# A diffusion backbone's last stage on one core: the half of the tokens that it begins with, and where a norm's sums stand among the last products

## Chip, core and metric

One core of a Trainium2 chip runs the whole kernel. The metric is the device time in microseconds (us), the median of several runs; the profile is one further execution. The engines are named TensorE (PE in the rows), VectorE (DVE), ScalarE (ACT), GpSimd (POOL) and SyncE (SP, which here only issues DMAs). Each engine takes its instructions strictly in the order in which the program gives them, and waits at one whose inputs are not there.

## What is computed

One layer of the backbone over 1024 tokens of 1024 channels: an adaptive norm, a two-directional diagonal state-space scan with a gate, and then the squared-ReLU MLP and a final norm, which is all that the change touches:

```python
def _rmsnorm(x, g):
    xf = x.astype(jnp.float32)
    y = xf * lax.rsqrt(jnp.mean(xf * xf, axis=-1, keepdims=True) + EPS)
    return (y * g.astype(jnp.float32)).astype(x.dtype)

def _mlp(h, w1, b1, w2, b2):
    a = jax.nn.relu(h @ w1 + b1)
    return (a * a) @ w2 + b2

# in reference(), D_FF = 4096:
        x = x + g2 * _mlp(_modulate(_rmsnorm(x, norm2_g[i]), sh2, sc2),
                          mlp_w1[i], mlp_b1[i], mlp_w2[i], mlp_b2[i])
    return _rmsnorm(x, final_g)
```

## The kernel before

Channels lie on the 128 partitions, in eight blocks `d`, tokens along the free dimension. `acc[:, d]` holds the running result x of block d for all 1024 tokens; `halves` are tokens 0 to 511 and 512 to 1023. Every float32 product is made of three matmuls (`mm3`, lines 783 to 785) of operands split in a rounded part and a rest: rounded x rounded, rounded x rest, rest x rounded. ScalarE makes the rounded part (`rounded`, line 937), VectorE or GpSimd subtracts to get the rest (`rest`, line 934).

The order of the work is written out by hand: the schedule is manual, and what the program lists first an engine does first.

The MLP's second product has 32 blocks of 128 hidden channels. The first 30 go through a seven-product scheme (Strassen's), in 70 steps, `t` = 0 to 69, of the loop at line 1444. Step t takes u = t // 14, one of seven products i and a quarter q of the output channels. Its parts:

- `y_rests(t)`: VectorE's rests of the activations that were rounded in step t - 1, among them, in steps 66 and 67, the rests of the weights `w2_last(0)` and `w2_last(1)` (128x1024 each).
- `product2(t)`: 18 matmuls of 512 columns, nine into the PSUM bank 2t mod 8 and nine into the next.
- `after2(t)`: VectorE takes the two banks into `acc` (`add_out`, line 1364) and, for some i, into a sum M or M into `acc`. For u = 4 that is four VectorE instructions at i = 0, 1, 3 and 5, two at i = 2 and 6, six at i = 4. The last steps are t = 62, 63 (i = 3), 64, 65, 66 (i = 4, 5, 6 of quarter 0) and 67, 68, 69 (i = 4, 5, 6 of quarter 1). Products i = 5 and 6 add to the first half of the tokens alone, so steps 68 and 69 no longer touch the second half.
- `beside(t)`: the loads (SyncE), the rounding for later steps (ScalarE), GpSimd's rests and sums of the weights. `plan(t, g, t_load)` puts an activation block g into these lists: loaded in step t_load, rounded in t, its rest in t + 1. Blocks 105 to 108 are the last two blocks of hidden channels, 105 and 106 for the first half of the tokens (`aa`), 107 and 108 for the second (`ab`).

The last stage, from line 1451 on, does the other two hidden blocks directly and the final norm:

- `m2_(toks, ds, aa)` makes, for each channel block d, six matmuls into a bank and one VectorE instruction (line 1463) that adds the bank to `acc`. `m2_sq` does that for each d and has ScalarE square the result (line 978) and VectorE or GpSimd add the square to a sum (line 979). Squares and adds are 512 columns wide for a half, 256 for a quarter of the tokens.
- `norm_cols` sums over the partitions by tiny matmuls (line 1001), and VectorE and ScalarE turn the sums into reciprocal roots with a Newton step (lines 1004 to 1013): one VectorE instruction, the root on ScalarE, four VectorE instructions. It is a generator: nothing is issued before its first `next`, which issues all up to the root.
- `norm_rows` spreads the roots over the partitions by matmuls into a PSUM bank (line 1019).
- `last` scales a block by gain and root on VectorE (line 1479) and, every second block, has SyncE issue the store (line 1475). For the last quarter ScalarE applies the gain (line 1516) ahead of time, and VectorE multiplies by the root (line 1520).

The order before: the first half is done whole (512 columns), with its adds on VectorE; then comes the third quarter of the tokens, with the first half's norm made beside it and the adds on GpSimd; then the fourth quarter, with the first half's eight `last` between its pieces; then the third quarter's eight `last`; then the fourth quarter's norm and store.

Of the kernel before, what the change touches and what calls it, by code (L numbers as in the profile page):

```python
# [47 lines left out]
def kernel(ctx, tc, cst, bc, x, xl, ada_w, glu_w, w1, w2, out):  # L48
# [41 lines left out]
    def bank(i, n=512, o=0):  # L90
        return PS[:, 512 * i + o:512 * i + o + n]
# [690 lines left out]
    def mm3(o, wt, xt, start, stop):  # L782
        PE.matmul(o, wt[0], xt[0], start=start, stop=False)  # L783
        PE.matmul(o, wt[0], xt[1], start=False, stop=False)  # L784
        PE.matmul(o, wt[1], xt[0], start=False, stop=stop)  # L785
# [146 lines left out]
    def rest(to, src, eng=V, *dims):  # L932
        hi, lo = (vw(v[:, 0:size(dims)], *dims) for v in to) if dims else to
        eng.tensor_tensor(lo, src, hi.bitcast(F32), op=OP.subtract)  # L934

    def rounded(to, src, *dims):
        S.copy(vw(to[0][:, 0:size(dims)], *dims) if dims else to[0], src)  # L937
# [34 lines left out]
    def sum_sq(d, toks, eng=None):  # L972
        n, ss = toks.stop - toks.start, sq_sum(toks)
        if d == 0:
            S.activation(ss, acc[:, d, toks], AF.Square)
        else:
            sq = tmp()[:, 0:n]
            S.activation(sq, acc[:, d, toks], AF.Square)
            (eng or P).tensor_tensor(ss, ss, sq, op=OP.add)
# [16 lines left out]
    def norm_cols(b, toks=halves[0]):  # L996

        n, ss = (toks.stop - toks.start) // 128, sq_sum(toks)
        cols = bank(b, n)
        for c in range(n):  # L1000
            PE.matmul(cols[:, c:c + 1], ss[:, 128 * c:128 * c + 128], one, start=True, stop=True)
        v, r, t = (C("ldt")[:, 12 * nn[0] + 4 * i:12 * nn[0] + 4 * i + n] for i in range(3))
        nn[0] += 1
        V.tensor_scalar(v, cols, 1.0 / D, EPS, op0=OP.mult, op1=OP.add)
        S.activation(r, v, AF.Sqrt)
        yield r
        V.reciprocal(r, r)
        yield
        V.scalar_tensor_tensor(t, v, -0.5, r, op0=OP.mult, op1=OP.mult)
        yield  # L1010
        V.tensor_tensor(t, t, r, op=OP.mult)
        yield
        V.scalar_tensor_tensor(r, t, 1.5, r, op0=OP.add, op1=OP.mult)
# [288 lines left out]
    def w2_last(f):  # L1302
        o = 1024 + 2048 * f
        return at(W, o, 1024), at(W, o + 1024, 1024)
# [4 lines left out]
    def plan(t, g, t_load):  # L1309
        loads.setdefault(t_load, []).append(g)  # L1310
        rounds.setdefault(t, []).append(g)
        rests.setdefault(t + 1, []).append(g)
# [5 lines left out]
            t = 14 * (u - 1)  # L1318
            plan(t + 8 + 2 * m // 3, 21 * u + m, t + (1, 2, 4, 6, 8, 12, 13)[0 if m < 5 else 1 + (m - 5) // 3])
    for m in range(4):  # L1320
        plan(66 + m // 2, 105 + m, 64)

    def beside(t):

        for g in loads.get(t, ()):
            load_y(g)
        if t == -6:
            load_w2(0, range(3, 4))
        elif t == -5:
            load_w2(1, (0, 2, 3, 1))  # L1330
        elif t in (-2, 0):
            i = t // 2 + 1
            SP.dma_start(out=acc[:, 6 + i], in_=RD[0].rearrange("(p a c) -> p a c", p=128, a=2)[:, i])
        round2(t + 3)
        for g in rounds.get(t, ()):
            to = y_slot(g)
            rounded(to, to[1].bitcast(F32))
        if t in (65, 66):
            rounded(w2_last(t - 65), w2_raw[:, t - 65])
        rest2(t + 3)  # L1340
        sum2(t + 4)
        if t == 62:
            SP.dma_start(out=w2_raw, in_=w2v[:, 30:32])

    def y_rests(t):
        for g in rests.get(t, ()):
            to = y_slot(g)
            rest(to, to[1].bitcast(F32))
        if t in (66, 67):
            rest(w2_last(t - 66), w2_raw[:, t - 66])  # L1350

    def bank2(p, n):
        return bank((2 * p + n) % 8)

    def product2(p):
        u, q, i = L2[p]
        hi, lo = (vw(v, 3, 2, 128) for v in slot2(p))
        for n in range(2):
            for m in range(3):
                mm3(bank2(p, n), (hi[:, m, n], lo[:, m, n]), y_slot(21 * u + 3 * i + m), m == 0, m == 2)  # L1360

# [4 lines left out]
    def after2(p):  # L1366
        u, q, i = L2[p]
        for n in range(2):
            d, o = 2 * q + n, bank2(p, n)
            m = at(M, 512 * d, 512)  # L1370
            if i == 0 and u == 0:
                S.copy(m, o)
            elif i in (0, 2):
                V.tensor_tensor(m, m, o, op=OP.add)
            for r, hf in (((0, 0),), ((0, 1), (1, 1)), (), ((0, 1),), ((1, 1), (1, 0)), ((0, 0),), ((1, 0),))[i]:
                add_out(o, d + 4 * r, hf)
            if u == 4 and i in (3, 4, 5):
                add_out(m, d + 4 * (i > 3), (1, 1, 0)[i - 3])
# [61 lines left out]
            S.activation(acc[:, b - 3], acc[:, b - 3], AF.Identity, bias=g2b2[:, b - 3:b - 2])  # L1440


    M = sp.tile([128, 2048], F32, name="M", tag="r2_7")
    for t in range(len(L2)):
        y_rests(t)
        product2(t)
        after2(t)
        beside(t)


    first, toks = halves[0], (slice(512, 768), slice(768, 1024))

    def m2_(toks, ds, aa, o_=0):
        w = [w2_last(f) for f in range(2)]
        n = toks.stop - toks.start
        ts = slice(o_, o_ + n)
        for f in range(2):
            for d in ds:
                ds_ = slice(128 * d, 128 * d + 128)
                mm3(bank(4 + d % 4, n), (w[f][0][:, ds_], w[f][1][:, ds_]), (aa[f][0][:, ts], aa[f][1][:, ts]), f == 0, f == 1)  # L1460
        for d in ds:
            o = acc[:, d, toks]
            V.scalar_tensor_tensor(o, bank(4 + d % 4, n), g2[:, d:d + 1], o, op0=OP.mult, op1=OP.add)  # L1463

    def m2_sq(toks, ds, aa, o_=0, eng=None):

        for d in ds:
            m2_(toks, [d], aa, o_)
            if d:
                sum_sq(d - 1, toks, eng)  # L1470
        if d == 7:
            sum_sq(7, toks, eng)
# [9 lines left out]

    ring = places[:3]
    aa, ab = ([y_slot(105 + 2 * hf + f) for f in range(2)] for hf in range(2))
    m2_sq(first, range(8), aa, eng=V)
    m2_(toks[0], range(4), ab)
    n1 = norm_cols(1, first)
    r_ = next(n1)
    for d in range(8):
        if d > 3:  # L1490
            m2_(toks[0], [d], ab)
        sum_sq(d, toks[0])
        next(n1, 0)
        if d == 5:
            rb = norm_rows(r_, 2, first)
    n1 = norm_cols(1, toks[0])
    for d in range(8):
        m2_sq(toks[1], [d], ab, 256)
        last(d, first, rb)
        if d == 2:  # L1500
            r_ = next(n1)
        elif d > 2:
            next(n1, 0)
    rb = norm_rows(r_, 3, toks[0])
    for d in range(4):
        last(d, toks[0], rb)
    n1 = norm_cols(1, toks[1])
    r_ = next(n1)
    last(4, toks[0], rb)
    for _ in n1:  # L1510
        pass
    for d in range(5, 8):
        last(d, toks[0], rb)
    for d in range(8):
        o = acc[:, d, toks[1]]
        S.activation(o, o, AF.Identity, scale=C("fg")[:, d:d + 1])
# [67 lines left out]
```

## Time and profile before

| what | us |
|---|---|
| median of 3 runs (1076.04 to 1077.04) | 1076.48 |
| the profiled execution: its own time | 1074.8 |
| the profiled execution: its span, first to last instruction | 1073.0 |
| busy in the span: TensorE | 954.5 |
| busy in the span: VectorE | 884.0 |
| busy in the span: GpSimd | 599.7 |
| busy in the span: ScalarE | 552.9 |

The share of busy time is a mean over stages with different limits, so the end of the span is to be read by itself: for every engine its instructions in order of time, and for each the idle time before it and what ended that. A row gives the start in us from the span's start, the duration, the engine, the line of the kernel, the operation, the result and its operands by tile name (T holds `acc` and the small vectors, PS is PSUM, UT the sum of squares, W and z the split activations and weights), the shapes, and a count where equal neighbours are merged; then the whole stretch is given. An instruction's duration reaches some 0.08 us into the next one on VectorE, and a matmul's even further, so that the step from start to start is the price of one in a run of equals.

### The profile page before, as it was taken

How to read it: one execution, taken by the hardware profiler on the slowest of the kernel's cores; microseconds unless marked ns; L12 is line 12 of the kernel's file. 1: busy time of each engine (PE TensorE's matmuls, PEld its weight loads, DVE VectorE, ACT ScalarE, POOL GpSimd, SP SyncE). 2: the span in 40 equal slices, each digit the busy share in tenths (PEclk: the TensorE clock that was granted, in tenths of full speed). 3: DMA queues.
4: the chain of work that ended last, by engine and by line, in shares of the span. 5: the costliest groups of instructions: out<-in, count | busy, mean ns of one | idle time of the engine just before them, and what ended most of it. 6: DMA issues, size and time to landing. Idle time of an engine off the chain costs nothing.

```text
span 1073.0 us, 15268 instructions
## 1 busy us (share of the span) xinstructions
PE 954.5 (89%) x5276; PEld 783.5 (73%) x5276; DVE 884.0 (82%) x1393; ACT 552.9 (52%) x1015; POOL 599.7 (56%) x411
## 2 busy tenths in 40 slices
PE   4788895656999998899999999998999999999995
PEld 4466674446888776588888888886678888888875
DVE  8799998999946776978665656656899999999997
ACT  6367683346973466656565554545444334343413
POOL 2868999735653814264232232324888787878603
PEclk9969797777999988999999999999999999999998
DMA  9514554775778211165545344469363535451204
GB/s 384 216 46 154 186 155 117 194 212 144 227 243 284 66 40 59 49 207 188 184 138 178 126 162 152 138 203 329 121 224 103 194 120 177 133 162 40 79 1 157
DMA packets 104782, 168.85 MB, mean 157 GB/s; under 512 B 7681, under 2 KB 61953, under 8 KB 103425
## 3 DMA queue, kind: packets, MB, share of 16 engines
q1 hardware_dynamic: 100272, 153.20, 43.6%
q10 hardware_dynamic: 4432, 14.68, 4.1%
q8 instruction: 41, 0.67, 0.3%
q14 instruction: 37, 0.29, 0.1%
HBM read 120.40 MB, written 47.45 MB: 156 GB/s over the span
## 4 chain that ended last, share of the span: by engine, by line
PE 54%; DVE 24%; ACT 8%; issue 5%; POOL 4%; DMA 4%; SPq 1%; DVEq 0%; ACTq 0%; POOLq 0%
PE PS L784 15%; PE PS L785 15%; PE PS L783 15%; DVE T L1364 3%; DVE X L476 2%; PE PS L154 2%; DVE X L475 2%; DMA DY<-X 1%; DVE z L934 1%; DVE PS L474 1%; DVE PS L473 1%; DVE W L934 1%; DVE PS L710 1%; PE PS L573 1%; PE PS L495 1%
## 5 line engine op out<-in xcount | busy, mean ns | idle before, releaser
L783 PE MATMUL PS<-z,W 128*128 128x512 f32 (+1 forms) x432 | 168.6, 390 | 2.9 <-DVE T L1184 1.5
L784 PE MATMUL PS<-z,W 128*128 128x512 f32 (+1 forms) x432 | 167.5, 388 | 2.5 <-DVE z L934 2.5
L785 PE MATMUL PS<-z,W 128*128 128x512 f32 (+1 forms) x404 | 156.7, 388 | 1.3 <-POOL W L934 1.2
L1364 DVE SCALAR_TENSOR_TENSOR T<-PS,T 128x512 f32<-128x512 f32 x160 | 112.1, 739 | 2.4 <-PE PS L785 2.2
L783 PEld LDWEIGHTS PS<-z,W 128*128 128x128 f32 x432 | 81.7, 189 | 21.2 <-DVE T L1463 2.2
L784 PE MATMUL PS<-W 128*128 128x512 f32 (+1 forms) x244 | 93.9, 385 | 3.4 <-DVE W L934 3.2
L784 PEld LDWEIGHTS PS<-z,W 128*128 128x128 f32 x432 | 81.7, 189 | 19.8 <-DVE z L934 3.7
L783 PE MATMUL PS<-W 128*128 128x512 f32 (+1 forms) x244 | 93.3, 382 | 0.0
L785 PEld LDWEIGHTS PS<-z,W 128*128 128x128 f32 x404 | 76.3, 189 | 17.9 <-POOL W L934 2.1
L934 DVE TENSOR_TENSOR z<-z 128x512 fp32r<-128x512 f32 x60 | 81.2, 1378 | 6.0 <-ACT z L937 6.0
L785 PE MATMUL PS<-W 128*128 128x512 f32 (+1 forms) x216 | 82.7, 383 | 1.5 <-POOL W L934 1.5
L785 PE MATMUL PS<-z,A 128*128 128x512 f32 x208 | 81.3, 391 | 2.5 <-POOL A L934 2.5
L934 DVE TENSOR_TENSOR W<-W 128x512 fp32r<-128x512 f32 x49 | 74.2, 1537 | 7.2 <-ACT W L937 7.2
L1212 POOL TENSOR_TENSOR T<-T 128x512 f32<-128x512 f32 x27 | 39.2, 1453 | 68.8 <-ACT T L1155 60.7
L785 PE MATMUL PS<-W,A 128*128 128x512 f32 x184 | 71.7, 390 | 0.3 <-POOL A L934 0.3
L783 PE MATMUL PS<-z,A 128*128 128x512 f32 x180 | 70.2, 390 | 0.0
L784 PE MATMUL PS<-z,A 128*128 128x512 f32 x180 | 70.0, 389 | 0.0
L1184 DVE TENSOR_TENSOR T<-T,PS 128x512 f32<-128x512 f32 x64 | 42.9, 685 | 32.4 <-PE PS L785 31.6
L937 ACT CAST W<-T 128x512 fp32r<-128x512 f32 (+1 forms) x46 | 33.0, 718 | 65.2 <-POOL T L1283 46.2
L937 ACT CAST W<-UT 128x512 fp32r<-128x512 f32 (+2 forms) x50 | 35.7, 714 | 58.6 <-POOL UT L1283 37.7
L495 PE MATMUL PS<-X,E 128*64 128x160 f32 x256 | 50.4, 339 | 14.5 <-DVE X L457 8.2
L783 PE MATMUL PS<-W,A 128*128 128x512 f32 x156 | 60.7, 389 | 0.0
(330 smaller groups left out, 2725.1 us busy)
## 6 DMA issues: line engine op xcount, KB each, us to landing
YD<-T SPq DMA_DIRECT2D x88, 256.0 KB, 2.3
z<-YD SPq DMA_DIRECT2D x60, 256.0 KB, 3.6
W<-YD SPq DMA_DIRECT2D x49, 256.0 KB, 4.2
T<-in_w_dram SPq DMA_DIRECT2D x9, 1024.0 KB, 5.8
T<-in_ada_w_dram ACTq DMA_DIRECT2D x17, 512.0 KB, 4.0
UT<-in_w_dram SPq DMA_DIRECT2D x8, 1024.0 KB, 5.9
T<-in_w_dram SPq DMA_DIRECT2D x20, 384.0 KB, 3.4
UT<-in_w_dram SPq DMA_DIRECT2D x15, 384.0 KB, 4.2
```

The costliest lines, as they stand in the source:

```text
L154: PE.matmul(ssq, C("sel"), a[:, g], start=(j, g) == (0, 0), stop=(j, g) == (7, 7))
L475: lambda: eng.tensor_tensor(out_, out_, ta, op=OP.add),
L476: lambda: eng.tensor_tensor(out_, out_, tb_, op=OP.add)]
L495: PE.matmul(b[0:64, c], e[:, g, c, 0:64], uj[:, g], start=True, stop=True)
L783: PE.matmul(o, wt[0], xt[0], start=start, stop=False)
L784: PE.matmul(o, wt[0], xt[1], start=False, stop=False)
L785: PE.matmul(o, wt[1], xt[0], start=False, stop=stop)
L934: eng.tensor_tensor(lo, src, hi.bitcast(F32), op=OP.subtract)
L937: S.copy(vw(to[0][:, 0:size(dims)], *dims) if dims else to[0], src)
L1184: V.tensor_tensor(to, x_, o, op=OP.add)
L1212: P.tensor_tensor(o, x_, z_, op=op)
L1364: V.scalar_tensor_tensor(o, src, g2[:, d:d + 1], o, op0=OP.mult, op1=OP.add)
```

## The change

The last stage takes the second half of the tokens whole and the first half in two quarters, and its start moves ahead of steps 68 and 69 of the second product. The adds to the sum of squares of the half stay on VectorE, those of the quarters on GpSimd. The column sums of the half's norm are issued between the two nine-matmul groups of step 68, the rest of its chain after step 68's product, its rows between the two groups of step 69. The half's eight `last` stand thus: one ahead of the first quarter, four among its pieces, one among those of the second quarter, two behind it. For this the weights' and the second half's activations are loaded, rounded and split earlier, and banks are numbered anew. No instruction of any engine is added or removed but for the order; the same matmuls, additions, squares and stores are issued. The diff:

```diff
@@ -1318,7 +1318,7 @@
             t = 14 * (u - 1)
             plan(t + 8 + 2 * m // 3, 21 * u + m, t + (1, 2, 4, 6, 8, 12, 13)[0 if m < 5 else 1 + (m - 5) // 3])
     for m in range(4):
-        plan(66 + m // 2, 105 + m, 64)
+        plan(64 if m > 1 else 66, 105 + m, 60)
     def beside(t):
@@ -1335,8 +1335,8 @@
         for g in rounds.get(t, ()):
             to = y_slot(g)
             rounded(to, to[1].bitcast(F32))
-        if t in (65, 66):
-            rounded(w2_last(t - 65), w2_raw[:, t - 65])
+        if t in (64, 65):
+            rounded(w2_last(t - 64), w2_raw[:, t - 64])
         rest2(t + 3)
         sum2(t + 4)
         if t == 62:
@@ -1346,16 +1346,18 @@
         for g in rests.get(t, ()):
             to = y_slot(g)
             rest(to, to[1].bitcast(F32))
-        if t in (66, 67):
-            rest(w2_last(t - 66), w2_raw[:, t - 66])
+        if t in (65, 66):
+            rest(w2_last(t - 65), w2_raw[:, t - 65])
     def bank2(p, n):
         return bank((2 * p + n) % 8)
-    def product2(p):
+    def product2(p, between=None):
         u, q, i = L2[p]
         hi, lo = (vw(v, 3, 2, 128) for v in slot2(p))
         for n in range(2):
+            if n and between:
+                between()
             for m in range(3):
                 mm3(bank2(p, n), (hi[:, m, n], lo[:, m, n]), y_slot(21 * u + 3 * i + m), m == 0, m == 2)
@@ -1440,27 +1442,20 @@
             S.activation(acc[:, b - 3], acc[:, b - 3], AF.Identity, bias=g2b2[:, b - 3:b - 2])
-    M = sp.tile([128, 2048], F32, name="M", tag="r2_7")
-    for t in range(len(L2)):
-        y_rests(t)
-        product2(t)
-        after2(t)
-        beside(t)
-
-
-    first, toks = halves[0], (slice(512, 768), slice(768, 1024))
+    second, toks = halves[1], (slice(0, 256), slice(256, 512))
     def m2_(toks, ds, aa, o_=0):
         w = [w2_last(f) for f in range(2)]
         n = toks.stop - toks.start
         ts = slice(o_, o_ + n)
+        b = [bank((4, 5, 0, 1)[d % 4] if n == 512 else 5 + d % 3, n) for d in range(8)]
         for f in range(2):
             for d in ds:
                 ds_ = slice(128 * d, 128 * d + 128)
-                mm3(bank(4 + d % 4, n), (w[f][0][:, ds_], w[f][1][:, ds_]), (aa[f][0][:, ts], aa[f][1][:, ts]), f == 0, f == 1)
+                mm3(b[d], (w[f][0][:, ds_], w[f][1][:, ds_]), (aa[f][0][:, ts], aa[f][1][:, ts]), f == 0, f == 1)
         for d in ds:
             o = acc[:, d, toks]
-            V.scalar_tensor_tensor(o, bank(4 + d % 4, n), g2[:, d:d + 1], o, op0=OP.mult, op1=OP.add)
+            V.scalar_tensor_tensor(o, b[d], g2[:, d:d + 1], o, op0=OP.mult, op1=OP.add)
     def m2_sq(toks, ds, aa, o_=0, eng=None):
@@ -1482,35 +1477,56 @@
     ring = places[:3]
     aa, ab = ([y_slot(105 + 2 * hf + f) for f in range(2)] for hf in range(2))
-    m2_sq(first, range(8), aa, eng=V)
-    m2_(toks[0], range(4), ab)
-    n1 = norm_cols(1, first)
-    r_ = next(n1)
+
+
+
+    M = sp.tile([128, 2048], F32, name="M", tag="r2_7")
+    def cols2():
+        n1.append(norm_cols(3, second))
+        r_.append(next(n1[0]))
+
+    def rows2():
+        rb.append(norm_rows(r_[0], 4, second))
+
+    n1, r_, rb = [], [], []
+    for t in range(len(L2)):
+        y_rests(t)
+        product2(t, {68: cols2, 69: rows2}.get(t))
+        if t == 68:
+            for _ in n1[0]:
+                pass
+        after2(t)
+        beside(t)
+        if t == 67:
+            m2_sq(second, range(8), ab, eng=V)
+    rb = rb[0]
+    last(0, second, rb)
     for d in range(8):
-        if d > 3:
-            m2_(toks[0], [d], ab)
-        sum_sq(d, toks[0])
-        next(n1, 0)
-        if d == 5:
-            rb = norm_rows(r_, 2, first)
+        m2_sq(toks[0], [d], aa)
+        if d < 4:
+            last(d + 1, second, rb)
     n1 = norm_cols(1, toks[0])
     for d in range(8):
-        m2_sq(toks[1], [d], ab, 256)
-        last(d, first, rb)
+        m2_sq(toks[1], [d], aa, 256)
         if d == 2:
             r_ = next(n1)
         elif d > 2:
             next(n1, 0)
-    rb = norm_rows(r_, 3, toks[0])
-    for d in range(4):
-        last(d, toks[0], rb)
+        if d == 4:
+            last(5, second, rb)
+    rb0 = norm_rows(r_, 3, toks[0])
+    last(6, second, rb)
+    last(7, second, rb)
+    for d in range(2):
+        last(d, toks[0], rb0)
     n1 = norm_cols(1, toks[1])
     r_ = next(n1)
-    last(4, toks[0], rb)
+    for d in range(2, 5):
+        last(d, toks[0], rb0)
     for _ in n1:
         pass
     for d in range(5, 8):
-        last(d, toks[0], rb)
+        last(d, toks[0], rb0)
     for d in range(8):
         o = acc[:, d, toks[1]]
         S.activation(o, o, AF.Identity, scale=C("fg")[:, d:d + 1])
```

## Rows read from the trace of the kernel before

**Rows 1.** Windows from 1047.17: length, engines' busy us (xcount), granted clock, DMA share, GB/s.

```profile
1047.17:1063.00 15.83, 12.51 (x102) 11.91 (x100) 13.51 (x37) 6.54 (x18) 10.04 (x14) 1.00 0.27 100
1063.00:1073.00 10.00, 2.23 (x8) 1.85 (x8) 6.11 (x20) 3.39 (x9) 0.24 (x1) 0.50 0.77 262
```

**Rows 2.** VectorE's timeline, steps 65 to 68 of the second product.

```profile
1020.61 0.75 DVE L1364 SCALAR_TENSOR_TENSOR T<-PS,T 128x512 f32<-128x512 f32 x1
...
1023.25 1.22 DVE L934 TENSOR_TENSOR W<-UT,W 128x1024 fp32r<-128x1024 f32 x1
1024.39 1.41 DVE L1364 SCALAR_TENSOR_TENSOR T<-PS,T 128x512 f32<-128x512 f32 x2
...
1028.04 1.40 DVE L1364 SCALAR_TENSOR_TENSOR T<-PS,T 128x512 f32<-128x512 f32 x2
...
1032.00 0.68 DVE L934 TENSOR_TENSOR z<-z 128x512 fp32r<-128x512 f32 x1
```

**Rows 3.** TensorE's timeline: start of step 67, of the last stage, first wait.

```profile
1019.46 0.39 PE L783 MATMUL PS<-z,A 128*128 128x512 f32 x1
...
1031.70 0.39 PE L783 MATMUL PS<-z,W 128*128 128x512 f32 x1
...
1037.96 0.50 PE L783 MATMUL PS<-z,W 128*128 128x512 f32 x1 [0.67 <-DVE T L1463]
```

**Rows 4.** VectorE's timeline, last stage, around the first half's norm.

```profile
1037.17 2.06 DVE L1463 SCALAR_TENSOR_TENSOR T<-PS,T 128x512 f32<-128x512 f32 x3
...
1047.09 1.65 DVE L1463 SCALAR_TENSOR_TENSOR T<-PS,T 128x256 f32<-128x256 f32 x4
1048.66 0.16 DVE L1004 TENSOR_SCALAR T<-PS 128x4 f32<-128x4 f32 x1
...
1049.80 0.89 DVE L1463 SCALAR_TENSOR_TENSOR T<-PS,T 128x256 f32<-128x256 f32 x2
1051.84 0.48 DVE L1463 SCALAR_TENSOR_TENSOR T<-PS,T 128x256 f32<-128x256 f32 x1 [1.16 <-PE PS L785]
1052.56 0.48 DVE L1463 SCALAR_TENSOR_TENSOR T<-PS,T 128x256 f32<-128x256 f32 x1 [0.24 <-PE PS L785]
```

**Rows 5.** TensorE's timeline: column sums (line 1001) and rows (line 1019).

```profile
1047.68 0.95 PE L1001 MATMUL PS<-T,UT 128*128 128x1 f32 x8
...
1050.00 1.09 PE L1019 MATMUL PS<-T 128*128 128x128 f32 x8
...
1063.30 1.01 PE L1001 MATMUL PS<-T 128*128 128x1 f32 x4 [1.06 <-POOL T L979]
```

**Rows 6.** VectorE's timeline: line 1479, the last norm, line 1520.

```profile
1054.74 0.74 DVE L1479 SCALAR_TENSOR_TENSOR T<-T,PS 128x512 f32<-128x512 f32 x1
...
1064.35 0.16 DVE L1004 TENSOR_SCALAR T<-PS 128x2 f32<-128x2 f32 x1 [0.26 <-PE PS L1001]
...
1066.94 2.74 DVE L1520 TENSOR_TENSOR T<-T,PS 128x256 f32<-128x256 f32 x8 [0.20 <-PE PS L1019]
```

**Rows 7.** GpSimd's timeline of the third quarter's adds.

```profile
1049.76 6.38 POOL L979 TENSOR_TENSOR T<-T 128x256 f32<-128x256 f32 x8 [35.62 <-ACT T L978]
```

**Rows 8.** TensorE's timeline and a window, around an earlier idle stretch.

```profile
377.64 2.07 PE L1019 MATMUL PS<-T 128*128 128x128 f32 x8 [4.07 <-DVE T L1013]
...
379.32:382.73 3.41, 3.41 (x10) 2.73 (x10) 2.08 (x4) 2.25 (x4) 0.00 (x0) 0.50 0.02 5
```

**Rows 9.** SyncE's and ScalarE's timelines: last loads, last weights' rounding.

```profile
1001.74 0.38 SPq L1343 DMA_DIRECT2D UT<-in_w_dram  x1
1002.23 1.50 SPq L1260 DMA_DIRECT2D z<-YD  x3
...
1007.74 1.05 ACT L937 CAST W<-UT 128x1024 fp32r<-128x1024 f32 x1
```

**Rows 10.** GpSimd's and VectorE's timelines, where both work on SBUF.

```profile
1007.18 4.10 POOL L934 TENSOR_TENSOR A<-T,A 128x768 fp32r<-128x768 f32 x2 [0.95 <-PE PS L785]
...
1009.50 2.93 DVE L934 TENSOR_TENSOR W<-W 128x512 fp32r<-128x512 f32 x2
```

## The prediction, made before the changed kernel was run

> **What bounds the kernel now.** The page's busy shares (TensorE 954.5 of 1073.0 us) say little here, since all that moves lies in the last 55 us. I read the windows of that stretch first, then VectorE's timeline, then TensorE's, each time looking for idle time and its releaser.
>
> Up to 1031.70 TensorE never pauses: from the start of step 67 at 1019.46 to the last stage's first matmul there are 54 matmuls in 12.24 us, 0.2267 each, 4.08 per step [rows 3]. So step 67's product is done at 1023.54, step 69's at 1031.70. VectorE takes step 67's banks only from 1028.04, 4.5 us after they were ready [rows 2]. It is behind, and it stays the engine that sets the pace: its first eviction of the last stage is at 1037.17 [rows 4], 5.5 us after TensorE began that stage, and TensorE has to wait for it at 1037.96 [rows 3]. In 1047.17 to 1063.00 VectorE is busy 13.51 of 15.83 us [rows 1]. Its largest pause is 1.16 us at 1051.84 [rows 4]. The last norm is a chain without cover, column sums at 1063.30 [rows 5] to the last eight products, which end at 1069.68 [rows 6]; the stores that follow give the span's end at 1073.0, 3.3 us later. Work on VectorE is thus the clock of the last stage, and the question is how long it stands idle in the new order.
>
> **The change part by part.** Nothing is removed: the same instructions run in another order, so the sum is one of VectorE's idle time.
>
> *Loads and rounding moved ahead.* The four loads of activations are issued at 1002.23, right behind the weights' load at 1001.74, and the weights are rounded from 1007.74 [rows 9]. Moved by four steps the loads go ahead of the weights' load in SyncE's queue. Their places were last read in step 55, long over by then, so nothing waits behind them. On ScalarE three more casts come before step 68's operand, and GpSimd's rest for it moves by about 1 us; TensorE needs it 12 us later. Zero.
>
> *Rests moved ahead.* On VectorE two activation rests (0.605 each) and the first weight rest (1.14, from 1023.25 to 1024.39) move ahead of `after2(65)`, the second weight rest ahead of `after2(66)` [rows 2]. The total up to `after2(67)` grows by the two activation rests, 1.2 us, which stood behind it at 1032.00. So the second half's first eviction comes at 1032.00 + 1.2 = 1033.2; the same follows from 1037.17 minus `after2(68)` (four at 0.66) and `after2(69)` (two), 3.96 in all.
>
> *TensorE's new wait.* After step 67 (1023.54) the last stage's first bank is bank 4, which is step 66's. Its eviction in `after2(66)` now stands behind 1020.61 + 1.2 + 1.14 + 2.64 + 1.14, and ends at about 1027.4. TensorE idles 3.9 us; steps 68 and 69 are queued behind. It then makes d = 0 to 3 in 1.36 us each, until 1032.9, before VectorE wants them: no cost at the full clock.
>
> *Evictions and adds of the half.* Eight evictions and seven adds took from 1037.17 to 1047.17, and at the same pace last from 1033.2 to 1043.2. TensorE gets step 68's first bank when d = 6 is evicted, at 1040.5, and is through its nine matmuls at 1042.5, so it waits for the last add. So far level: VectorE has left out 3.96 us of work and is 3.96 us earlier.
>
> *Column sums.* Before, four evictions of the third quarter (1.6 us from 1047.09) lay between the last add and the norm's first VectorE instruction at 1048.66 [rows 4], over the eight tiny matmuls of 0.95 us [rows 5]. Now the instruction behind the last add is that one, and it waits: 1043.2 plus 0.95 plus the semaphores is 1044.2, **1.1 us idle**. The covering product is on TensorE, and VectorE, the late engine, has nothing to cover it. The chain behind (1048.66 to 1049.80, 1.14) costs the same in both orders: until 1045.4.
>
> *Steps 68 and 69.* TensorE goes on at 1044.0: second group of 68 (9 x 0.2267 = 2.04), first group of 69 (2.04), the rows (0.85 of 1.09 before the next matmul can start [rows 5]), second group of 69 (2.04): 1051.0, in PSUM at 1051.15. VectorE needs from 1045.4 only 2.64 for `after2(68)`, so it waits 0.2 for the first bank of 69 and, at 1048.95, **2.2 us** for the second. Six instructions of `after2` meet 7.0 us of TensorE. `last` is queued behind them. VectorE leaves `after2(69)` at 1051.8; the same work was done at 1047.09 + 1.14 = 1048.2 before. **3.6 us lost.**
>
> *The rest.* From 1051.8: one `last` (0.66), four pairs of eviction (0.40) and `last`: 1056.7. Then twelve quarter evictions have one `last` among them, and VectorE falls to TensorE's 0.72 a piece (1051.84 to 1052.56 [rows 4]): four waits of 0.3. The third norm instruction waits for GpSimd: its seven adds at 0.8 (1049.76, eight in 6.38 [rows 7]) begin with a squared piece every 1.05 us, and end at 1060.9; column sums 0.5 to 0.8; idle 1.0, and twice some 0.3 behind. The next quarter's adds follow at 0.8 and end at 1067.7, so the last norm starts at 1068.6, where VectorE waited 0.85. Before it was 1064.35 [rows 6]. Three `last` blocks now stand between its first instruction and the rest, three behind, and the final eight start at about 1071.7 instead of 1066.94 [rows 6], and end at 1074.4. Idle time in this part is 4.3 us; the same reckoning of the old order has 2.7. **1.6 us lost.**
>
> *Stores.* Before, 2.5 MB are issued in the last 7 us; now it's the same (one pair of half-width blocks, then eight quarter pairs), so I keep the 3.3 us at the end. In the last 10 us the DMA engines were busy 0.77 of the time [rows 1].
>
> The sum is 1.1 + 2.4 + 1.6 = 5.1; with its rounding kept 5.2. Done with the same prices for the old order, from 1037.17 on, the reckoning ends VectorE's last instruction at 1069.3, where the trace has 1069.68, so its own error is some 0.4 us.
>
> *The clock.* The 3.9 us of TensorE's idle time have one near likeness in the trace: 4.07 us before the rows at 377.64, behind which the granted clock is 0.50, that is 1.2 GHz, with ten matmuls in 3.41 us [rows 8]. At that pace d = 0 to 3 take 2.57 each instead of 1.36; if it holds for some 7 us from 1027, d = 2 and 3 come late to VectorE and 0.7 us are lost; for half of that time nothing is. I take 0.3. The range takes 0 to 2.4.
> The Trainium skill ("TensorE: Matmul & The Clock Gate", section "HAM oscillation — how this bites in real kernels") says that waits between groups of matmuls throttle the engine so that each next group starts cold; the trace agrees, with the 0.50 behind the 4.07 us [rows 8]. By that rule every pause of the new order would be a danger; the pauses after 1033 are of 1 us or less, and in the old order pauses such as TensorE's 0.67 at 1037.96 [rows 3] left the clock at 1.00 up to 1063 [rows 1].
>
> The profiled execution of before took 1074.8 with a span of 1073.0; the median of the runs is 1.7 above. I add the difference to the median: 1076.5 + 5.2 + 0.3 = **1082.0**.
>
> **The rivals.**
> *The clock stays low (slower still).* If the half clock of [rows 8] is granted also in 1043 to 1050, the 7.0 us between the last add and step 69's second bank become some 10: plus 2.9, thus about 1084.6. For it speaks that TensorE pauses at 1033, 1039.5 and 1042.5 too; against it that it is busy some nine tenths between. Chance 0.13.
>
> *VectorE isn't behind (faster).* Its delay comes in part from GpSimd: two rests at 1009.50 take 2.93 us while GpSimd works from 1007.18 to 1011.28 [rows 10], where two take 1.21 alone [rows 2]. With the casts in a new order GpSimd's two rests have a gap between them. Were all such slow instructions of this stretch free, up to 4.9 us would go, and the second half's first eviction would come with TensorE, near 1028.5. Then the sum is 5.2 - 4.9 = 0.3, the waits of the last part fall by 1.6 as GpSimd and TensorE are ahead, and the last norm's tiny matmuls, now at clock 0.50 [rows 1] with 1.01 us for four [rows 5] where eight took 0.95, win 0.9: 1074.3. It decides when VectorE begins the half before 1028.8. Against it: GpSimd's work isn't less, and only its last two rests move. Chance 0.07.
> The Trainium skill ("SBUF — State Buffer", section "Who interferes with whom") says that VectorE with two SBUF inputs contends with a GpSimd instruction that reads SBUF, and that the issue order decides who blocks; by that rule a small shift could free VectorE of the whole wait, and the trace agrees that there is one, 2.93 against 1.21.
>
> *No difference.* Had the two waits on TensorE been covered as the placement suggests, that is, were VectorE to have 3.5 us of other work while the column sums and step 69 run, 3.6 us would go, and with half of the last part's loss too it is 1077.7. The order is fixed by hand, and no such work stands there. Chance 0.06.
>
> **How the numbers follow.** The forecast has 0.74, the low clock 0.13, the faster case 0.07, no difference 0.06. The forecast's own spread is 1079.3 (VectorE's delay 2.5 us less by part of the GpSimd effect) to 1084.4 (clock 2.4 above the sum). The range goes on to the low clock's 1084.6 and a bit: 1079.0 to 1085.2; the two other cases stay out. About 0.2%, 2 us, is what a measurement of this kernel can tell from no change: slower 0.87, same 0.06, faster 0.07.
>
> **What would show it.** Right: TensorE idle for nearly 4 us ahead of the last stage's first matmul; the first eviction of line 1463 at about 1033 of the span; an idle of about 1 us before the first norm instruction of four columns, released by the column sums; one of 2 us or more before the last `add_out` of step 69, released by line 785; the last line 1520 group some 5 us later. Wrong: if VectorE is without idle time from the half's evictions to its `last`, the central step is wrong; if the granted clock is 0.50 for more than 7 us in that stretch, the size is; if the half's evictions begin before 1029, the delay was not carried along.

## The result, and the profile after

The changed kernel takes 1082.38 us (median of 5, 1081.79 to 1085.59) where the kernel before takes 1076.48 (median of 5, 1074.11 to 1077.49): a ratio of 1.0065, 95% interval 1.0044 to 1.0086. It is slower by some 5.9 us (the interval reaches from 4.7 to 9.3). The page's head:

```profile
span 1080.0 us, 15272 instructions
PE 956.1 (89%) x5276; PEld 783.5 (73%) x5276; DVE 885.6 (82%) x1393; ACT 553.2 (51%) x1015; POOL 598.8 (55%) x411
```

The engines are as busy as before, within 2 us, and the span is 7.0 us longer. Not all of that belongs to the change: the same point ahead of it, VectorE's first eviction of step 64, comes at 1016.65 in the profile of before and at 1018.08 in that of after, and among the profiles of the experiments below anywhere from 1015.70 to 1021.19 (but for e12, which changes what lies ahead of it), in kernels that are nearly alike up to there. So everything that follows is measured from that eviction to the end of VectorE's last eight products, called the **stage**. Its start in the kernel before (its end is in [rows 6], 1066.94 + 2.74 = 1069.68):

```profile
1016.65 1.41 DVE L1364 SCALAR_TENSOR_TENSOR T<-PS,T 128x512 f32<-128x512 f32 x2
```

The stage is 53.03 us before. It repeats far better than the time: the kernels below whose stage did not change agree in it within 0.05 us, while their spans differ by up to 5, so it tells apart what the medians can't. VectorE's timeline after (start, duration, engine, line, operation; in brackets the idle time before and what ended it; L1366 is `add_out`, L1458 the eviction of a piece, that is of one channel block's six matmuls, L979 the adds, L1004 to L1013 a norm's instructions, L1474 `last`, L1536 the last eight products):

```profile
1018.08 1.41 DVE L1366 SCALAR_TENSOR_TENSOR T<-PS,T 128x512 f32<-128x512 f32 x2
...
1034.64 2.06 DVE L1458 SCALAR_TENSOR_TENSOR T<-PS,T 128x512 f32<-128x512 f32 x3
...
1043.96 0.69 DVE L979 TENSOR_TENSOR UT<-UT,T 128x512 f32<-128x512 f32 x1 [0.16 <-ACT T L978]
1045.79 0.17 DVE L1004 TENSOR_SCALAR T<-PS 128x4 f32<-128x4 f32 x1 [1.15 <-PE PS L1001]
...
1046.92 0.75 DVE L1366 SCALAR_TENSOR_TENSOR T<-PS,T 128x512 f32<-128x512 f32 x1
...
1050.04 0.75 DVE L1366 SCALAR_TENSOR_TENSOR T<-PS,T 128x512 f32<-128x512 f32 x1 [0.39 <-PE PS L785]
1053.01 0.75 DVE L1366 SCALAR_TENSOR_TENSOR T<-PS,T 128x512 f32<-128x512 f32 x1 [2.22 <-PE PS L785]
1053.68 0.74 DVE L1474 SCALAR_TENSOR_TENSOR T<-T,PS 128x512 f32<-128x512 f32 x1
...
1060.08 0.48 DVE L1458 SCALAR_TENSOR_TENSOR T<-PS,T 128x256 f32<-128x256 f32 x1 [0.29 <-PE PS L785]
...
1063.54 0.16 DVE L1004 TENSOR_SCALAR T<-PS 128x2 f32<-128x2 f32 x1 [0.71 <-PE PS L1001]
1064.36 0.48 DVE L1458 SCALAR_TENSOR_TENSOR T<-PS,T 128x256 f32<-128x256 f32 x1 [0.66 <-PE PS L785]
...
1066.61 0.47 DVE L1011 TENSOR_TENSOR T<-T 128x2 f32<-128x2 f32 x1
...
1067.39 0.69 DVE L1013 SCALAR_TENSOR_TENSOR T<-T 128x2 f32<-128x2 f32 x1
...
1070.55 0.16 DVE L1004 TENSOR_SCALAR T<-PS 128x2 f32<-128x2 f32 x1
...
1073.93 2.74 DVE L1536 TENSOR_TENSOR T<-T,PS 128x256 f32<-128x256 f32 x8 [0.21 <-PE PS L1019]
```

The stage is 1073.93 + 2.74 - 1018.08 = 58.59, **5.56 longer**. Its first eviction of a piece (L1458) comes 16.56 after its start, where it was 20.52 before [rows 4]; the 4 us that it is earlier are lost again in the waits at 1045.79, 1050.04 and 1053.01, which are all for TensorE, and more behind them. TensorE's timeline and the windows after (length; busy time with counts of TensorE, its weight loads, VectorE, ScalarE, GpSimd; granted clock; DMA share, GB/s):

```profile
1029.05 0.47 PE L783 MATMUL PS<-z,W 128*128 128x512 f32 x1 [3.92 <-DVE T L1366]
...
1030.74 0.63 PE L783 MATMUL PS<-z,W 128*128 128x512 f32 x1
...
1033.30 0.55 PE L783 MATMUL PS<-z,W 128*128 128x512 f32 x1
...
1041.99 0.50 PE L783 MATMUL PS<-z,A 128*128 128x512 f32 x1 [0.16 <-DVE T L1458]
...
1044.70 1.05 PE L1001 MATMUL PS<-T,UT 128*128 128x1 f32 x8 [0.37 <-DVE UT L979]
...
1066.92 0.28 PE L785 MATMUL PS<-z,W 128*128 128x256 f32 x1
```

```profile
1026.00:1029.00 3.00, 0.00 (x0) 0.00 (x0) 3.00 (x5) 0.00 (x0) 0.00 (x0) 1.00 0.00 0
1029.00:1032.00 3.00, 2.95 (x9) 2.38 (x10) 3.00 (x6) 0.00 (x0) 0.00 (x0) 0.70 0.00 0
1032.00:1035.00 3.00, 3.00 (x11) 2.42 (x10) 3.00 (x6) 0.00 (x0) 0.00 (x0) 0.73 0.00 0
1035.00:1038.00 3.00, 3.00 (x15) 2.47 (x14) 2.90 (x5) 1.86 (x3) 0.00 (x0) 1.00 0.00 0
```

and, before, the first matmul behind the half's eight pieces and the last matmul of a piece:

```profile
1043.54 0.28 PE L783 MATMUL PS<-z,W 128*128 128x256 f32 x1
...
1059.45 0.28 PE L785 MATMUL PS<-W 128*128 128x256 f32 x1
```

TensorE stands idle for 3.92 us ahead of the half's first piece, runs some of the next matmuls at half clock, 1.2 GHz (six take 2.56 us from 1030.74 on, where they take 1.36 at 2.4 GHz; the two windows that hold them are granted 0.70 and 0.73 on average), and gets to step 68 at 1041.99. It had been ready at 1025.1 (1029.05 less 3.92), and the eight pieces are 10.9 us of matmuls: 6.0 us of its time are gone. In the old order the same eight pieces cost it 1.0 (from 1031.70 [rows 3] to 1043.54). That is 5.0 more; its last piece, 42.8 us into the stage before (1059.45), comes at 48.84 after, 6.0 later, so that about 1 us more is lost behind the half's pieces. The end comes 9.75 behind that piece's last matmul instead of 10.23: 5.56 later.

### The profile page after: what moved, and what is told of

It reads as the page before. It is cut to its first block, busy times and chain, and to the rows that moved or that the text cites. A ratio compares the mean times of both kernels' runs of the same rounds, so it can differ in the third digit from the quotient of the medians.

```text
span 1080.0 us, 15272 instructions
## 1 busy us (share of the span) xinstructions
PE 956.1 (89%) x5276; PEld 783.5 (73%) x5276; DVE 885.6 (82%) x1393; ACT 553.2 (51%) x1015; POOL 598.8 (55%) x411
## 4 chain that ended last, share of the span: by engine, by line
PE 53%; DVE 26%; ACT 6%; issue 5%; DMA 5%; POOL 3%; SPq 1%; DVEq 0%; ACTq 0%; POOLq 0%
PE PS L785 15%; PE PS L784 15%; PE PS L783 15%; DVE T L1366 2%; DVE X L476 2%; PE PS L154 2%; DVE X L475 2%; DVE PS L474 2%; DVE PS L473 2%; DVE z L934 1%; DVE W L934 1%; DMA DY<-X 1%; SPq L595 1%; ACT T L735 1%; DVE PS L710 1%
## 5 line engine op out<-in xcount | busy, mean ns | idle before, releaser
L783 PE MATMUL PS<-z,W 128*128 128x512 f32 (+1 forms) x440 | 170.7, 388 | 5.7 <-DVE T L1366 3.9
L784 PE MATMUL PS<-z,W 128*128 128x512 f32 (+1 forms) x440 | 169.4, 385 | 2.5 <-DVE z L934 2.5
L785 PE MATMUL PS<-z,W 128*128 128x512 f32 (+1 forms) x412 | 158.7, 385 | 1.3 <-POOL W L934 1.2
L1366 DVE SCALAR_TENSOR_TENSOR T<-PS,T 128x512 f32<-128x512 f32 x160 | 112.2, 739 | 5.0 <-PE PS L785 4.8
L783 PEld LDWEIGHTS PS<-z,W 128*128 128x128 f32 x440 | 83.8, 190 | 24.0 <-issue 4.3
L784 PEld LDWEIGHTS PS<-z,W 128*128 128x128 f32 x440 | 83.7, 190 | 19.7 <-DVE z L934 3.7
L784 PE MATMUL PS<-W 128*128 128x512 f32 x236 | 93.5, 396 | 4.7 <-DVE W L934 4.7
L783 PE MATMUL PS<-W 128*128 128x512 f32 x236 | 92.9, 394 | 0.0
L785 PEld LDWEIGHTS PS<-z,W 128*128 128x128 f32 x412 | 78.1, 190 | 17.6 <-POOL W L934 2.1
L785 PE MATMUL PS<-W 128*128 128x512 f32 x208 | 82.3, 396 | 1.5 <-POOL W L934 1.5
L937 ACT CAST W<-T 128x512 fp32r<-128x512 f32 (+1 forms) x46 | 33.0, 718 | 63.1 <-POOL T L1283 42.5
```

The costliest lines, as they stand in the source:

```text
L1366: V.scalar_tensor_tensor(o, src, g2[:, d:d + 1], o, op0=OP.mult, op1=OP.add)
```

## The experiments

**More work for TensorE or for VectorE, in either order (e8 to e11).** These four say which engine the stage waits for at the place where the work is put; nothing uses its results. In the changed kernel, six more matmuls in step 69 (e8):

```diff
     def rows2():
         rb.append(norm_rows(r_[0], 4, second))
+        for m in range(2):
+            mm3(bank(6), (w2_last(0)[0][:, :128], w2_last(0)[1][:, :128]), ab[0], True, True)
```

> The changed kernel with six more matmuls of 512 columns (about 1.36 us of TensorE) between the rows and the second group of step 69. The stage is measured from VectorE's first eviction of step 64 to the end of the last eight products: 53.0 us in the kernel before, 58.6 in the changed one. If TensorE is what the stage waits for there (it lost its lead before step 68): 58.6 + 1.4 = 60.0. If VectorE's work alone set the length and the waits were incidental: 58.6.

```profile
1052.62 0.75 DVE L1366 SCALAR_TENSOR_TENSOR T<-PS,T 128x512 f32<-128x512 f32 x1 [3.58 <-PE PS L785]
```

The wait for step 69's second bank grows from 2.22 to 3.58, by just the 1.36 us, and the stage is 60.32, 1.73 longer; another 0.39 is a wait at the last norm's start that was not there. The same lines ahead of `m2_sq(first, ...)` in the kernel before, into bank 5 with `aa[0]` (e9):

> The kernel before with the same six matmuls ahead of the last stage's first matmul. If TensorE has a lead there that hides them: 53.0, no change. If TensorE's work counts in the old order too: 54.4.

The stage is 52.99: nothing. The first piece is evicted 20.51 us into it, as before. Two more additions on VectorE in the changed kernel (e10); `after2(t, ns)` takes only the banks of step t that `ns` names:

```diff
-    def after2(p):
+    def after2(p, ns=range(2)):
...
-        for n in range(2):
+        for n in ns:
...
-        after2(t)
+        after2(t, range(1 if t == 69 else 2))
+        if t == 69:
+            for m in range(2):
+                V.tensor_tensor(at(UT, 0, 512), at(UT, 512, 512), at(UT, 1024, 512), op=OP.add)
+            after2(t, (1,))
```

> The changed kernel with two more VectorE additions of 128x512 (0.6 us each) between the two banks of step 69. If VectorE only waits there (2.2 us): 58.6, and the wait in the trace shrinks to about 1.0. If VectorE sets the length: 59.8.

```profile
1056.10 0.75 DVE L1366 SCALAR_TENSOR_TENSOR T<-PS,T 128x512 f32<-128x512 f32 x1 [0.89 <-PE PS L785]
```

The wait shrinks from 2.22 to 0.89 and the stage is 58.58: nothing. The same two ahead of the last stage in the kernel before (e11):

> The kernel before with the same two additions behind step 69's evictions, ahead of the last stage's first eviction. If VectorE is the late engine there: 53.0 + 1.2 = 54.2. If TensorE sets the length: 53.0.

The stage is 54.30, 1.27 longer: paid in full. So the late engine is VectorE ahead of the old order's last stage, and TensorE in step 69 of the new order. The change has swapped them.

**The wait for the column sums, covered (e1).** With `after2(p, ns)` as above:

```diff
...
     def cols2():
+        after2(68, (0,))
         n1.append(norm_cols(3, second))
         r_.append(next(n1[0]))
...
-        after2(t)
+        after2(t, (1,) if t == 68 else range(2))
```

> The changed kernel, but step 68's first bank (two VectorE instructions, 1.3 us) is evicted ahead of the norm's first VectorE instruction, so that the 1.15 us of waiting for the column sums have cover. Stage in the changed kernel 58.6. By the prediction's sum, in which each idle stretch of VectorE is a term of its own: 58.6 - 1.1 = 57.5. If TensorE's chain from the last add over steps 68 and 69 sets the end: 58.6, the wait only moves to step 69's banks, which then wait about 1.1 longer.

```profile
1043.81 0.16 DVE L1004 TENSOR_SCALAR T<-PS 128x4 f32<-128x4 f32 x1
...
1045.87 0.75 DVE L1366 SCALAR_TENSOR_TENSOR T<-PS,T 128x512 f32<-128x512 f32 x1 [0.86 <-PE PS L785]
...
1047.91 0.75 DVE L1366 SCALAR_TENSOR_TENSOR T<-PS,T 128x512 f32<-128x512 f32 x1 [0.63 <-PE PS L785]
1050.88 0.75 DVE L1366 SCALAR_TENSOR_TENSOR T<-PS,T 128x512 f32<-128x512 f32 x1 [2.22 <-PE PS L785]
```

The norm's first instruction no longer waits, and the stage is 58.54: nothing won. The idle time is found again at the second bank of 68 (0.86) and the first of 69 (0.63, before 0.39), and the 2.22 stay. Up to step 69's second bank VectorE can be no earlier than TensorE's banks.

**The wait of step 69, filled (e2).** Three `last` stand between step 69's two evictions, the other five behind pieces 2 and 4 of the first quarter and 1, 3 and 5 of the second; `after2(p, ns)` as above:

```diff
...
-        after2(t)
+        if t == 69:
+            after2(t, (0,))
+            for d in range(3):
+                last(d, second, rb[0])
+            after2(t, (1,))
+        else:
+            after2(t)
...
-    last(0, second, rb)
...
-        if d < 4:
-            last(d + 1, second, rb)
+        if d in (2, 4):
+            last(3 if d == 2 else 4, second, rb)
...
-        if d == 4:
-            last(5, second, rb)
+        if d in (1, 3, 5):
+            last(5 + d // 2, second, rb)
...
-    last(6, second, rb)
-    last(7, second, rb)
```

> The changed kernel, but three of the half's blocks of line 'last' stand between step 69's two evictions, where VectorE waited 2.2 us, and the other five are spread over the quarters' pieces. By the sum of VectorE's idle terms: 2.2 there and about 1 in the last part, 58.6 - 3.2 = 55.4. If TensorE's chain sets the end: the sixteen pieces can't come sooner than TensorE makes them, and only some 1.4 is won: 57.2.

```profile
1049.11 0.75 DVE L1366 SCALAR_TENSOR_TENSOR T<-PS,T 128x512 f32<-128x512 f32 x1 [0.34 <-PE PS L785]
1050.00 2.06 DVE L1474 SCALAR_TENSOR_TENSOR T<-T,PS 128x512 f32<-128x512 f32 x3
1052.08 0.75 DVE L1366 SCALAR_TENSOR_TENSOR T<-PS,T 128x512 f32<-128x512 f32 x1
...
1066.56 0.87 DVE L1474 SCALAR_TENSOR_TENSOR T<-T,PS 128x256 f32<-128x256 f32 x2 [0.41 <-PE PS L1019]
1068.23 0.16 DVE L1004 TENSOR_SCALAR T<-PS 128x2 f32<-128x2 f32 x1 [0.80 <-PE PS L1001]
```

The 2.2 us are filled. The stage is 57.15: 1.44 won, as TensorE's chain gives, not 3.2. TensorE now makes all sixteen pieces with no longer pause than 0.42 us (for GpSimd's adds), and its last one comes at 47.30, 1.54 earlier. In the last part VectorE's waits did not shrink, as the sum had it; with those for the norms (0.41, 0.80) they came to 3.6 us in all, from 2.9. The time is 1.0038 of the kernel before (1.0024 to 1.0052).

**Sums and rows behind the products (e3).**

```diff
-        product2(t, {68: cols2, 69: rows2}.get(t))
+        product2(t)
+        if t > 67:
+            (cols2, rows2)[t - 68]()
```

> The changed kernel, but the column sums stand behind step 68's product and the rows behind step 69's, not between the groups. If the places in the middle are what makes the move bearable: slower, some 1 us above 58.6. If TensorE's order counts: in the middle the column sums hold the second group of 68 until the last add is there, and the rows hold the second group of 69; behind the products they do not, and the stage is 58.6 - 0.9 = 57.7.

```profile
1045.94 0.17 DVE L1004 TENSOR_SCALAR T<-PS 128x4 f32<-128x4 f32 x1 [2.55 <-PE PS L1001]
```

VectorE waits 2.55 for the column sums, more than twice as long, but no longer for any bank of 68 or 69, and the stage is 57.32, 1.27 shorter (0.9 were expected). The time is 1.0047 (1.0027 to 1.0067) of the kernel before. The two places in the middle, taken by themselves, cost: the sums hold 68's second group until VectorE's last add (0.37 us of TensorE at 1044.70), and the rows stand ahead of 69's second group (0.81 us). Which of them gave how much was not run.

**The pieces one step later (e6).** Behind step 68, the sums in the middle of 69, the rows behind it (and banks 4 to 7, the sums in bank 0, which the cut leaves out):

```diff
...
-        product2(t, {68: cols2, 69: rows2}.get(t))
-        if t == 68:
+        product2(t, {69: cols2}.get(t))
+        if t == 69:
             for _ in n1[0]:
                 pass
+            rows2()
...
-        if t == 67:
+        if t == 68:
             m2_sq(second, range(8), ab, eng=V)
```

> The changed kernel with the half's eight pieces behind step 68 instead of step 67, the column sums between the groups of step 69 and the rows behind its product. TensorE then keeps 4.1 us more of work while VectorE catches up. If TensorE's lost lead is the cause: its pause before the stage goes, and the stage is 58.6 - 2.0 = 56.6. If the loss comes from the uncovered norm alone: step 69 alone covers less than two steps, and the stage is 58.6 or longer.

```profile
1032.43 0.50 PE L783 MATMUL PS<-z,W 128*128 128x512 f32 x1 [0.16 <-DVE T L1366]
...
1038.38 0.50 PE L783 MATMUL PS<-z,W 128*128 128x512 f32 x1 [2.29 <-DVE T L1458]
```

The 3.92 us of idle time ahead of the pieces are gone; pauses of 0.16, 0.31 and 2.29 among them and one of 1.49 for the last add take their place, but step 68 is done by then. The stage is 56.89, 1.70 shorter (2.0 were expected); the time is 1.0045 (1.0031 to 1.0059) of the kernel before. Part of the lead is kept, and that part of the loss goes. The other 3.9 of the 5.56 us were not won back here; no run joins e2, e3 and e6, or puts the pieces behind step 69.

**The pause and the clock (e7).**

```diff
-        b = [bank((4, 5, 0, 1)[d % 4] if n == 512 else 5 + d % 3, n) for d in range(8)]
+        b = [bank((0, 1, 4, 5)[d % 4] if n == 512 else 5 + d % 3, n) for d in range(8)]
```

> The changed kernel, but the half's pieces begin with banks 0 and 1, which were free long before, not with 4 and 5, whose eviction TensorE waits 3.9 us for. The pause is then about 2 and 1 us, and the clock should not fall. If the pause and the 3.4 us at half clock behind it cost: 58.6 - 0.7 = 57.9. If VectorE's delay covers them, as the trace suggests: 58.6.

```profile
1028.35 0.50 PE L785 MATMUL PS<-W 128*128 128x512 f32 x1 [2.07 <-DVE W L934]
...
1035.49 0.50 PE L783 MATMUL PS<-z,W 128*128 128x512 f32 x1 [2.54 <-DVE T L1458]
```

```profile
1023.00:1038.00 15.00, 10.39 (x45) 7.97 (x44) 14.90 (x22) 1.86 (x3) 0.00 (x0) 1.00 0.00 0
```

The pause is cut in two (2.07 and 2.54; 2 and 1 were expected), the clock stays at 1.00, and the stage is 58.55: no difference. So the fall of the clock costs nothing. The pauses are moved, not removed: TensorE waits for VectorE in any case, a little earlier or later, and then 1.49 us for the last add, where it waited 0.37.

**One part of the change alone (e4, e5).** In the kernel before, the halves exchanged (`first = halves[1]`, the quarters those of the first half, `ab, aa` for `aa, ab`; e4):

> The kernel before with the two halves of the tokens exchanged in the last stage and nothing moved ahead: one part of the change alone. Stage 53.0 in the kernel before. If the order of the halves costs nothing: 53.0 within 0.3. If the order by itself costs: above 53.5.

The stage is 53.01. And in the kernel before, the loads, casts and rests moved ahead (the three edits of the diff in `plan`, `beside` and `y_rests`; e5):

> The kernel before with only the loads, casts and rests of the last two blocks moved ahead as in the change. By the prediction: no change, 53.0 within 0.3, the first eviction of the last stage as late behind step 64 as before (20.5 us). If moving them costs by GpSimd's and VectorE's use of SBUF together: the first eviction comes 0.5 us or more later.

The stage is 53.01 and its first piece is evicted at 20.52. Each part by itself costs nothing; what is left for the loss is the order of the pieces, steps 68 and 69, the norm and `last`.

**VectorE relieved in the old order (e12).** Since VectorE is late there, its six rests of the last two hidden blocks go to GpSimd:

```diff
-            rest(to, to[1].bitcast(F32))
+            rest(to, to[1].bitcast(F32), P if g > 104 else V)
         if t in (66, 67):
-            rest(w2_last(t - 66), w2_raw[:, t - 66])
+            rest(w2_last(t - 66), w2_raw[:, t - 66], P)
```

> The kernel before with the six rests of the last two hidden blocks (four of 128x512, two of 128x1024, together 4.7 us of VectorE) on GpSimd, which has nothing to do from step 65 to the last stage. If VectorE is the late engine of the old order and TensorE has a lead: the last stage's first eviction comes 4.7 us earlier less what VectorE's additions of M lose beside GpSimd (four of them, up to 0.8 us each), and the stage is 53.0 - 1.5 to 2.2 = 51.0, since beyond some 2.2 us TensorE's lead is used up. If the loss beside GpSimd eats the gain, or TensorE sets the length: 53.0 or more.

```profile
1012.05 5.15 DVE L934 TENSOR_TENSOR W<-W 128x512 fp32r<-128x512 f32 x2
...
1021.04 1.75 DVE L934 TENSOR_TENSOR z<-z 128x512 fp32r<-128x512 f32 x1
...
1040.92 0.75 DVE L1463 SCALAR_TENSOR_TENSOR T<-PS,T 128x512 f32<-128x512 f32 x1 [0.52 <-PE PS L785]
```

```profile
1022.85 0.50 PE L784 MATMUL PS<-z,W 128*128 128x512 f32 x1 [3.42 <-DVE z L934]
```

It is slower, 1.0021 (1.0004 to 1.0038). The rows tell why. VectorE is indeed relieved, so much that it waits for TensorE at 1040.92. But GpSimd, which goes straight on from 1009.73 to 1028, makes the three rests that step 66 needs take 5.15 us for two, where it was 2.93 [rows 10], and 1.75 for the third; TensorE waits 3.42 us for that one, and part of its lead is gone here too. Since this lies ahead of step 64's eviction, the kernel is measured from the first of these rests: 63.1 us to the end of the last eight products (1075.12), where it is 60.2 before (1009.50 to 1069.68).

## Why the prediction was right, point by point

**The size.** Forecast were 5.2 us from the order and 0.3 from the clock; measured are 5.56 in the stage and 5.9 between the medians, 1082.38 against 1082.0. That the medians agree to 0.4 is in part luck, since their difference is known only to be 4.7 to 9.3; the stage is the better measure, and in it the order alone cost 5.56. Two ends of the forecast's own spread were added up loosely: 2.4 for the clock in place of 0.3 makes 1084.1, not 1084.4, and 2.5 off the forecast 1079.5, not 1079.3.

**The rests and the first eviction.** Forecast at 1033.2, that is 16.6 behind step 64's first eviction; measured 16.56. Moving the loads, casts and rests costs nothing: shown by e5.

**TensorE's pause.** Forecast 3.9, measured 3.92, for the releaser that was named, L1366. That VectorE covers it holds for the clock and for where the pause stands (e7), but "no cost" hides the cause: over the eight pieces TensorE lost 6.0 us that it had been ahead, 5.0 more than before, and with step 68 in their place part of the loss goes (e6).

**The single waits.** 1.1 for the column sums (1.15), 0.2 and 2.2 for step 69's banks (0.39 and 2.22), up to 1051.8 (forecast 35.15 into the stage, measured 35.60). Up to here every wait stands where it was put.

**What was wrong in it** is the step from VectorE that "stays the engine that sets the pace" to a sum of VectorE's waits, each a loss by itself. VectorE sets the pace in the old order, ahead of the last stage (e11: paid, e9: free). In the new one it is TensorE from the half's last add to step 69's second bank (e8: paid, e10: free, e1). Behind that VectorE has no wait until 1060.08: there its own work counts again, and it is what e2 makes less. So the 1.1 are not a term that could be won back: covered, they reappear behind (e1). The 2.2, filled, and the other `last` spread out are worth 1.44 together, not 3.2 (e2). The sum came out right because it was made by following the order of both engines, in which TensorE's delay shows as VectorE's waits. The third case, "no difference", was priced on the same mistake: filling the waits one at a time won 0.05 (e1) and 1.44 (e2), far from 3.6 us; both together were not run.

**The last part.** Up to the end of step 69's evictions 3.6 were forecast as lost and 4.05 are (35.60 into the stage, where the like point before, the 1048.2 of the text, is 31.6). So 5.56 - 4.05 = 1.5 are left for the last part, against 1.6. Inside it two misses nearly cancel. VectorE was forecast to wait 0.85 for the last norm and didn't (1070.55), and, counted from step 69's evictions, it came there 0.9 later than forecast: the norm's tiny instructions at 1066.61 and 1067.39 took 0.47 and 0.69, where their like takes 0.16. GpSimd was at its adds:

```profile
1065.50 1.56 POOL L979 TENSOR_TENSOR T<-T 128x256 f32<-128x256 f32 x2 [0.36 <-ACT T L978]
1067.34 1.53 POOL L979 TENSOR_TENSOR T<-T 128x256 f32<-128x256 f32 x2 [0.28 <-ACT T L978]
```

That the overlap is the cause is argued from rows; no run took it away. But both end as a GpSimd add ends (1067.08 with the pair from 1065.50, 1068.08 about halfway through the pair from 1067.34), and in e2, where the adds fall otherwise, so do the lengthened ones (1063.84 and 1065.75; adds end at 1063.82 and 1065.73), while the one that began just ahead of an add (1064.19) stayed short:

```profile
1063.46 0.38 DVE L1009 SCALAR_TENSOR_TENSOR T<-T 128x2 f32<-128x2 f32 x1
...
1064.16 0.14 DVE L1011 TENSOR_TENSOR T<-T 128x2 f32<-128x2 f32 x1
...
1065.28 0.47 DVE L1013 SCALAR_TENSOR_TENSOR T<-T 128x2 f32<-128x2 f32 x1
```

**The clock.** It did fall behind the pause (0.70 and 0.73 in two windows of the changed kernel, then 1.00), and the 0.3 taken for it are not there: with the clock at 1.00 throughout the stage is the same (e7). By the two windows the half clock held for some 3.4 us, half of the 7 that the 0.7 were reckoned with, and for half of that time the prediction has nothing too. Its 2.57 a piece is right (2.56), though ten matmuls in 3.41 us would make 2.05 for six; the window's edges are counted among the ten. The rival with a clock that stays low did not come.

The rule of the Trainium skill that was cited ("TensorE: Matmul & The Clock Gate", section "HAM oscillation — how this bites in real kernels") is told there of a loop whose matmuls wait for a DMA at each turn, and not of every pause, as the prediction has it. The trace agrees for the pause of 3.92 us, whose cost was hidden behind VectorE's delay. Pauses of 2.07 and 2.54 (e7) and 2.29 (e6) left the clock at 1.00, but behind one of 2.04 in e11 it was 0.51, 1.2 GHz, for some 3 us. These runs do not show what makes the difference.

**The faster case** asked for VectorE to begin the half before 1028.8, that is 5.3 behind the end of step 67's product (1023.54). It began 9.5 behind it (1034.64 against 1025.13): with GpSimd's last two rests moved a little, VectorE's two rests beside them took 2.94, as before (2.93).

**Not settled:** why step 64 is reached anywhere within 5.5 us in different profiles. But for e12, what the runs change lies behind it, except the moved loads, casts and rests, and e5, which has these alone, reaches it earliest (1015.70). It was not tried.

## What to carry to other kernels

An engine that is ahead of the one that sets the pace holds a lead, and work that needs the late engine's results must not be put in front of work that does not: here eight pieces that wait for VectorE's banks were moved ahead of two steps that TensorE could have done meanwhile; it lost 6.0 us over them instead of 1.0, and the stage grew by 5.56. To see which engine a stretch waits for, add a microsecond of work to each in turn at that place: here it was paid on one and vanished on the other, in a single profile each. A wait of the engine that is not late is not a term of a sum: covered, it moved (e1), or gave only what the other engine's chain allowed (e2).

## What was not expected of the hardware

A VectorE instruction on 128x2 elements, 0.16 us alone, took 0.47 and 0.69 while GpSimd was at adds of 128x256, and ended with an add. Two 128x512 rests took 1.21 us alone, 2.93 beside one stretch of GpSimd, and 5.15 beside GpSimd working without a gap. The time up to the same instruction differs by several us among profiles of kernels that are nearly alike up to there, while the stretch of 53 us behind it repeats within 0.05 in those of the old order.
